# A hybrid decoder layer in fp32: another order of work on TensorE in the mLSTM stage, and a merge that VectorE adds

## The chip, the core and the metric

The kernel runs on one core of one Trainium2 chip. The metric is the time of one execution on the device in microseconds (us), as the median of several runs. The profile comes from one execution of its own, taken by the hardware profiler, with its own time.

The engines are named as the profile names them: PE is TensorE (matmuls; PEld is its weight load), DVE is VectorE, ACT is ScalarE, POOL is GpSimd, SP is SyncE, which issues most DMAs.

## The reference, cut to what matters

One layer on 512 tokens of width 1024. A normalised input feeds two branches, an mLSTM with four heads (branch a) and a sliding-window attention (branch b). Both are projected, gated and added; an output projection, an MLP and a gated embedding follow.

```python
h = rmsnorm(x, norm_mix_g[i])
proj = h @ w_in[i]
...
h_ml = mlstm_chunkwise(q_ml, k_ml, v_ml, ig, lf)          # 4 heads, 128 wide q and k, 256 wide v
h_ml = h_ml * lax.rsqrt(jnp.mean(h_ml * h_ml, axis=-1, keepdims=True) + EPS)
y_a = jax.nn.sigmoid(o_ml) * h_ml * mlstm_norm_g[i]
y_b = swa_with_sinks(q_sw, k_sw, v_sw, sinks[i])
merged = jax.nn.sigmoid(g_a) * (y_a @ w_branch_a[i]) + jax.nn.sigmoid(g_b) * (y_b @ w_branch_b[i])
x = x + merged @ w_out[i]
...
```

## The kernel before, in words

**Arithmetic.** Each fp32 operand of a large product is split into a high and a low part (`split`: ACT casts the high part, DVE subtracts it to get the low part), and the product is three matmuls: high by high, high by low, low by high (`pairs`). One tile of 128 weight columns against all 512 tokens is 8 row blocks times 3, so 24 matmuls of 128x512. One such matmul is called a piece below, the 24 together a column block. `load_w` loads a column block by a DMA of SP's queue and splits it; four pairs of split weights are held (`WB`).

**Stages.** The input projections come first, then the attention (16 units), then the mLSTM with the projection of branch b, then the projection of branch a with the merge, then the output projection, the MLP in four quarters, and the end. The change lies in the mLSTM stage, the merge and the first lines of the output projection.

**The end of the attention.** There PE's order is written out by hand (`manual_schedule` on PE): the last q and k projections are cut into pieces by a generator, and `more(n)` issues n of them between the attention's own products. The last k block ends there; ACT and DVE then run its causal convolution (L671, L673), and `silu` (ACT sigmoid L680, DVE multiply L681) finishes the q and k tiles of all four heads (`acc` in the trace).

**The mLSTM stage.** `ml_weights(h)` makes one head's masked, decayed scores, in four column groups s = 0 to 3 of 512, 384, 256 and 128 tokens. For each group, ACT takes exponentials of 128x128 slices (`dm`, L835, one slice of them from `dg`, which DVE makes at L814), PE makes the score product q by k (L842) in a PSUM bank, DVE multiplies the two (L843), and `split` makes the weights `wT`. `ml_out(h)` multiplies them with the values (`vh`) in four token blocks of 3, 6, 9 and 12 matmuls (30 in all, tile `pst`, L168), ACT copies each result out (L855), DVE takes the denominator (`hd`, `den`, `rd`), and ACT squares the results for the norm (`jk`, L864). `ml_norm` scales the head's result `hs` on DVE (L873) by a root that ACT takes (L259, with a table load before it). `ya_of(h)` turns two blocks of a head on PE (L894), gates them on DVE (`sy`, L895) and splits them into `ya`.

**PSUM.** In this stage PSUM has eight banks: `g` two tiles of a bank for the projections (`psg`), `t` two tiles of a bank (`pst`), `a` two tiles of two banks (`psa`). Scores, products with the values and turned blocks all share the two `t` tiles. A tile's next use waits until its last reader is done.

**Order.** Nothing fixes PE's order here: `branch_b(2h)`, `ml_weights(h+1)`, `ml_out(h)` and `branch_b(2h+1)` are written one after the other, and the framework's scheduler merges them by its own estimates of when each is ready. The order on ACT and DVE is the scheduler's in both kernels. Every engine runs its own list in order.

**Branch b, branch a and merge.** `branch_b(i)` is a column block against `yb`, gated by DVE into `t2[i]` (L882). After the heads, eight column blocks of branch a against `ya` follow; DVE gates each (L920), POOL adds `t2[i]` (L921), and `split` makes `mg`. Then a second set of PSUM tiles takes over the same eight banks: `pair` (three tiles of two banks) for the output projection, allocated first, and `g`.

Of the kernel before, what the change touches and what calls it, by code (L numbers as in the profile page):

```python
# [16 lines left out]
P = 128  # L17
# [20 lines left out]
def block_kernel(  # L38
# [601 lines left out]
    def gate_of(put, i):  # L640

        if i % 2 == 0:
            loaded[0] = sp.tile([P, 2, 512], F32, tag="pT", bufs=2, name=nm("gl"))
            nc.sync.dma_start(out=loaded[0], in_=put[i // 2])
        return loaded[0][:, i % 2, :]

    gbd = gate_proj(w_gb)
    gad = gate_proj(w_ga)
# [87 lines left out]
    def swa_out(kp, gp, n, pTs):  # L736
# [14 lines left out]
        for g in range(2):  # L751
# [5 lines left out]
                o.rearrange("p (m g c) -> p m g c", m=2, g=2)[:, :, g, :],  # L757
            )

    def pieces():  # L760

        order = [("k", 0), ("q", 4), ("q", 5), ("k", 4), ("q", 6), ("q", 7), ("k", 1), ("k", 5), ("k", 2), ("k", 6), ("k", 3), ("k", 7)]
        for kind, i in order:
            w = load_w((w_qsw if kind == "q" else w_qkml)[i], KT * P, KT)
            ps = ps_g()
            for k in range(KT):
                ops = pairs([t[:, k, :] for t in w], hT[k])
                for j, (l, r) in enumerate(ops):
                    T.matmul(ps, l, r, start=k == 0 and j == 0, stop=k == KT - 1 and j == 2)  # L769
                    yield  # L770
            (q_done if kind == "q" else qk_done)(i, ps)

    fill = pieces()

# [32 lines left out]
    def h_of(h, t):  # L807
        return hs[h][t // 2][:, (t % 2) * DV : (t % 2 + 1) * DV]

    def ml_weights(h):  # L810
        pr = sp.tile([P, 512], F32, tag="pr", bufs=2, name=nm("pr"))
        nc.sync.dma_start(out=pr, in_=rrd[h : h + 1, :].broadcast_to([P, 512]))
        dg = act_f("dg")
        V.tensor_tensor(  # L814
            dg.rearrange("p (t j) -> p t j", t=NT),
            pr.rearrange("p (t j) -> p t j", t=NT),
            tri.unsqueeze(1).broadcast_to([P, NT, P]),
            ALU.add,
        )
        if h < 2:  # L820
            room = bp.tile([P, KT, 512], F32R, tag="big", bufs=2, name=nm("wT"))
            w0, w1, l0, l1 = [room[:, k, :] for k in range(4)]
            w2 = [room[:, 4, : 2 * P], room[:, 4, 2 * P :]]
        else:
            w0, w1, l0, l1 = [act_r("wT") for _ in range(4)]
            w2 = [sp.tile([P, 2 * P], F32R, tag="vs", bufs=4, name=nm("wT")) for _ in range(2)]
        wT = [(w0, l0), (w1[:, : 3 * P], l1[:, : 3 * P]), w2, (w1[:, 3 * P :], l1[:, 3 * P :])]
        vhl = [head_values() for _ in range(2)]
        for s in range(NT):
            split([v[:, s, :] for v in vhl], vm[s][:, h, :])  # L830
            dm = act_f("dm")
            n0 = s * P
            for t in range(s, NT):
                src = dg if t == s else pr
                A.activation(  # L835
                    dm[:, t * P : (t + 1) * P],
                    src[:, t * P : (t + 1) * P],
                    AF.Exp,
                    bias=gc[:, t * NT + s, h : h + 1],
                )  # L840
            psc = ps_t()
            T.matmul(psc[:, n0:], qk[4 + h][:, n0 : n0 + P], qk[h][:, n0:], start=True, stop=True)  # L842
            V.tensor_mul(dm[:, n0:], psc[:, n0:], dm[:, n0:])  # L843
            split(wT[s], dm[:, n0:])
        wts[h] = wT, vhl

    def ml_out(h):
        wT, vhl = wts.pop(h)
        for t in range(NT):
            pn = ps_t()  # L850
# [3 lines left out]
            chain(pn[:, : DV + 2], ops, True, True)  # L854
            A.copy(h_of(h, t), pn[:, :DV])  # L855
            V.tensor_copy(hd[:, h, t : t + 1], pn[:, DV : DV + 1])
        den = small("den", NT, 2)
        V.scalar_tensor_tensor(den, hd[:, h, :], -1.0, hd[:, h, :], ALU.mult, ALU.max)
        V.tensor_max(den, den, gc[:, NT * NT :, h])
# [15 lines left out]

    t2 = [None] * 8

    def branch_b(i):
        ps = ps_g()
        mm_T(ps, load_w(w_b[i], KT * P, KT), yb)  # L880
        t2[i] = act_f("gb")
        V.tensor_mul(t2[i], ps, gate_of(gbd, i))  # L882

# [14 lines left out]
    ml_weights(0)  # L898
    rds = []
    for h in range(NH):  # L900
        branch_b(2 * h)
        if h + 1 < NH:
            ml_weights(h + 1)
        rds.append(ml_out(h))
        branch_b(2 * h + 1)
        if h == 1:
            ml_norm([0, 1], rds)
        elif h > 1:
            ml_norm([h], rds[h:])
            ya_of(h - 2)  # L910
    ya_of(2)
    ya_of(3)


    mg = []
    for i in range(8):
        ps = ps_g()
        mm_T(ps, load_w(w_a[i], KT * P, KT), ya)
        sg = act_f("sga")
        V.tensor_mul(sg, ps, gate_of(gad, i))  # L920
        G.tensor_tensor(sg, sg, t2[i], ALU.add)  # L921
        m_ = act_hl("mg")
        split(m_, sg)
        mg.append(m_)


    st_s.close()
# [12 lines left out]
    def ps_g():  # L940
        return pp.tile([P, 512], F32, tag="g", bufs=2, name=nm("psg"))

    def columns_of(dst, k, g):

        ps = pair()[:, 0, :]
        for m in range(NT):
            T.transpose(ps[:, m * P : (m + 1) * P], xk[m][:, k * P : (k + 1) * P], ident)  # L947
        split(dst[k], ps, g[:, k : k + 1])
# [3 lines left out]
    for nh in range(2):  # L952
# [361 lines left out]
```

## Time and profile before

| | |
|---|---|
| Time before, median of 3 runs | 897.93 us (896.87 to 898.82) |
| The profiled execution's own time | 897.05 us |
| Its span (first to last instruction) | 895.3 us |
| PE busy | 884.4 us, 99% of the span |
| DVE busy | 644.8 us, 72% |
| ACT busy | 450.1 us, 50% |
| POOL busy | 24.3 us, 3% |
| Mean granted clock of PE | 0.999 |

The span and the time differ by 1.75 us, which lie outside the instructions. Busy time of PE counts pipelined matmuls with a modelled end: a matmul of 512 columns is drawn 0.39 us long though the next one starts after 0.23 us. So a PE that is 99% busy is one with hardly any gaps, and the length of a stretch is read from starts, not from durations. Idle time that a row names stands in brackets behind it, with the instruction that ended it.

### The profile page before, as it was taken

What the parts mean: (1) busy time and instruction counts of PE and PEld (TensorE: products, weight loads), DVE (VectorE), ACT (ScalarE), POOL (GpSimd) and SP (SyncE); (2) the same over time, 40 slices, a digit from 0 to 9 for tenths busy, and PEclk for the clock granted to TensorE, in tenths of its full rate; (3) what the DMA queues carried; (4) which work ended last, traced back from release to release, by engine and by line L of the source; (5) the groups of instructions that cost most, each with busy time, mean ns of one, the idle gap of its engine ahead of it and who ended that gap; (6) DMA issues with size and microseconds to landing.
All of it is one profiled execution on the core that took longest, in us unless ns stands there. A gap on an engine that the chain in (4) does not pass through costs nothing.

```text
span 895.3 us, 12110 instructions
## 1 busy us (share of the span) xinstructions
PE 884.4 (99%) x4676; PEld 739.9 (83%) x4676; DVE 644.8 (72%) x1029; ACT 450.1 (50%) x757; POOL 24.3 (3%) x42
## 2 busy tenths in 40 slices
PE   9999999999999999999999999999999999999996
PEld 8888899998777777788878888888888888888886
DVE  6875687863877887667634679757966885798566
ACT  6463445443657577765322545334434533444843
POOL 1011000000000000001300000000000000000000
PEclk9999999999999999999999999999999999999999
DMA  7552234345202123335452520630252054102402
GB/s 285 189 176 83 70 118 143 141 137 170 71 24 72 48 94 119 98 114 166 140 189 95 213 70 25 208 109 36 86 197 94 1 169 158 50 25 73 139 1 95
DMA packets 29965, 100.50 MB, mean 112 GB/s; under 512 B 4173, under 2 KB 4685, under 8 KB 29906
## 3 DMA queue, kind: packets, MB, share of 16 engines
q1 hardware_dynamic: 27938, 93.15, 31.4%
q0 software_dynamic: 1824, 6.30, 2.0%
q8 instruction: 37, 0.61, 0.3%
q10 hardware_dynamic: 144, 0.26, 0.1%
q14 instruction: 22, 0.18, 0.1%
HBM read 91.30 MB, written 8.40 MB: 111 GB/s over the span
## 4 chain that ended last, share of the span: by engine, by line
PE 92%; DVE 4%; ACT 3%; issue 0%; POOL 0%; DVEq 0%; POOLq 0%
PE psg L168 45%; PE psp L168 23%; PE psa L168 10%; PE psg L769 4%; PE pst L168 3%; ACT lm L716 1%; PE psa L697 1%; PE psg L319 1%; PE psa L731 1%; DVE acc L673 1%; PE pst L842 1%; PE pst L744 1%; DVE lm L705 1%; PE psp L947 1%; DVE lm L720 1%; PE psg L247 1%
## 5 line engine op out<-in xcount | busy, mean ns | idle before, releaser
L139 ACT CAST wh<-wr 128x1024 fp32r<-128x1024 f32 x134 | 140.6, 1052 | 211.6 <-PE psg L168 61.7
L140 DVE TENSOR_TENSOR wl<-wr,wh 128x1024 fp32r<-128x1024 f32 x134 | 168.5, 1262 | 97.1 <-ACT wh L139 90.1
L168 PE MATMUL psg<-x,wh 128*128 128x512 f32 x512 | 158.3, 390 | 0.0
L168 PE MATMUL psp<-wh,uf 128*128 128x512 f32 x448 | 139.2, 390 | 0.0
L168 PEld LDWEIGHTS psg<-x,wh 128*128 128x128 f32 x512 | 96.1, 188 | 19.7
L168 PE MATMUL psg<-x,wl 128*128 128x512 f32 x256 | 99.7, 389 | 0.0
L168 PEld LDWEIGHTS psp<-wh,uf 128*128 128x128 f32 x448 | 84.1, 188 | 17.3
L168 PE MATMUL psp<-wl,uf 128*128 128x512 f32 x224 | 87.2, 389 | 0.0
L139 ACT CAST wh<-wd 128x1024 fp32r<-128x1024 f32 x44 | 46.3, 1054 | 57.4 <-PE psp L168 25.8
L769 PE MATMUL psg<-h,wh 128*128 128x512 f32 x192 | 61.6, 397 | 0.4 <-DVE acc L673 0.4
L140 DVE TENSOR_TENSOR wl<-wd,wh 128x1024 fp32r<-128x1024 f32 x44 | 53.4, 1218 | 4.4 <-ACT wh L139 4.1
L168 PEld LDWEIGHTS psg<-x,wl 128*128 128x128 f32 x256 | 48.1, 188 | 9.9
L168 PE MATMUL psa<-h,wh 128*128 128x256 f32 (+1 forms) x256 | 55.1, 311 | 0.0
L168 PEld LDWEIGHTS psp<-wl,uf 128*128 128x128 f32 x224 | 42.1, 188 | 8.7
L140 DVE TENSOR_TENSOR uf<-F,uf 128x1792 fp32r<-128x1792 f32 (+2 forms) x20 | 33.0, 1651 | 21.8 <-ACT uf L139 21.8
L168 PEld LDWEIGHTS psa<-h,wh 128*128 128x128 f32 x256 | 41.9, 191 | 3.5 <-ACT p L618 0.8
L168 PE MATMUL psg<-yb,wh 128*128 128x512 f32 x128 | 43.0, 408 | 0.3 <-DVE gb L882 0.2
L769 PEld LDWEIGHTS psg<-h,wh 128*128 128x128 f32 x192 | 35.6, 188 | 7.8 <-ACT pT L733 0.8
L716 ACT ACTIVATE lm<-lm,nmx 128x256 f32<-128x256 f32 (+1 forms) x64 | 30.0, 470 | 23.6 <-DVE nmx L709 23.6
L139 ACT CAST uf<-F 128x1792 fp32r<-128x1792 f32 (+2 forms) x20 | 27.9, 1397 | 26.3 <-DVE F L1023 26.2
L168 PE MATMUL psg<-ya,wh 128*128 128x512 f32 x128 | 40.6, 395 | 0.0
L1009 DVE SCALAR_TENSOR_TENSOR rt<-psg,rB 128x512 f32<-128x512 f32 x32 | 22.0, 689 | 25.6 <-PE psg L168 25.6
(289 smaller groups left out, 1745.1 us busy)
## 6 DMA issues: line engine op xcount, KB each, us to landing
wr<-in_w_up SPq DMA_DIRECT2D x32, 512.0 KB, 3.5
wd<-in_w_down SPq DMA_DIRECT2D x24, 512.0 KB, 4.3
wr<-in_w_o SPq DMA_DIRECT2D x8, 512.0 KB, 4.0
gd<-gr POOLq DMA_DIRECT2D x8, 512.0 KB, 3.4
wr<-in_w_qsw SPq DMA_DIRECT2D x8, 512.0 KB, 4.3
wr<-in_w_qkml SPq DMA_DIRECT2D x8, 512.0 KB, 3.3
wr<-in_w_b SPq DMA_DIRECT2D x8, 512.0 KB, 3.4
gl<-gd SPq DMA_DIRECT2D x8, 512.0 KB, 3.4
```

The costliest lines, as they stand in the source:

```text
L139: done = A.copy(dst[0], src)
L140: V.tensor_sub(dst[1], src, r32(dst[0]))
L168: last_mm[0] = T.matmul(ps, l, r, start=first and i == 0, stop=last and i == len(ops) - 1, skip_group_check=parts)
L247: tc.keep_in_program_order(T.matmul(idle[:, :P], ones, ones, start=True, stop=True))
L319: last_mm[0] = T.matmul(ps[:, :264], act, w, start=done == 0, stop=done == 3 * KT - 1)
L673: V.scalar_tensor_tensor(acc[:, s:], ps[:, : S - s], cw[:, i * 4 + 3 - s : i * 4 + 4 - s], acc[:, s:], ALU.mult, ALU.add)
L697: T.matmul(o, q[x][HALF[ab], n * P : (n + 1) * P], keys[kp][y][HALF[ab], k0 : k0 + 256], start=i == 0, stop=i == 2)
L705: V.tensor_tensor_reduce(lm3[:, g, :], ls[:, g * 256 : g * 256 + W], band[:, 256 - W :], 0.125, sk[:, g // 2, g % 2 : g % 2 + 1], ALU.add, ...
L716: A.activation(lm3[:, g, :], lm3[:, g, :], AF.Exp, bias=nmx[:, g : g + 1], accum_out=sm[:, g : g + 1])
L720: V.tensor_tensor(lm3, lm3, rc.unsqueeze(2).broadcast_to([P, 4, W]), ALU.mult)
L769: T.matmul(ps, l, r, start=k == 0 and j == 0, stop=k == KT - 1 and j == 2)
L1009: V.scalar_tensor_tensor(a, ps, 0.0, rB, ALU.max, ALU.mult)
```

## The change

The edit has four parts.

1. The mLSTM stage gets a written order on PE. The projection of branch b, and the first two column blocks of branch a, become a generator of 240 pieces (`branches`), which `more(n)` places between the heads' own products: 6 behind each score of head 0, 5 behind each score of the other heads, 4 behind each token block of an output, 8 behind the turned blocks of heads 0 and 1, 44 behind those of head 2, and the last 32 behind those of head 3. `ml_weights(0)` comes first, ahead of any piece.
2. The score products go to the `a` tiles (two tiles, of which one bank each is used) and no longer share the `t` tiles.
3. In the merge DVE adds the two branches (`a_done`), where POOL did.
4. The second set of PSUM tiles allocates its two `g` tiles first, so that they take the banks of the old `g` tiles and the `pair` tiles take the others. They serve the second half of the output projection.

The loaded gates are kept by their source, since branch a and b now alternate.

```diff
-    def ml_weights(h):
+    def ml_weights(h, n):
...
-            psc = ps_t()
+            psc = ps_a()[:, :512]
             T.matmul(psc[:, n0:], qk[4 + h][:, n0 : n0 + P], qk[h][:, n0:], start=True, stop=True)
             V.tensor_mul(dm[:, n0:], psc[:, n0:], dm[:, n0:])
             split(wT[s], dm[:, n0:])
+            more(n)
...
-    def branch_b(i):
-        ps = ps_g()
-        mm_T(ps, load_w(w_b[i], KT * P, KT), yb)
+    def branches():
+
+        for i in range(8):
+            yield from pieces_of(w_b[i], yb, lambda ps: b_done(i, ps))
+        for i in range(2):
+            yield from pieces_of(w_a[i], ya, lambda ps: a_done(i, ps))
...
+    def a_done(i, ps):
+        sg = act_f("sga")
+        V.tensor_mul(sg, ps, gate_of(gad, i))
+        V.tensor_add(sg, sg, t2[i])
+        mg.append(act_hl("mg"))
+        split(mg[i], sg)
+
+    fill = branches()
     rds = []
-    for h in range(NH):
-        branch_b(2 * h)
...
+    with tc.manual_schedule(engines={mybir.EngineType.PE}):
+        ml_weights(0, 6)
+        for h in range(NH):
+            if h + 1 < NH:
+                ml_weights(h + 1, 5)
+            rds.append(ml_out(h, 4))
+            if h == 1:
+                ml_norm([0, 1], rds)
+            elif h > 1:
+                ml_norm([h], rds[h:])
+                ya_of(h - 2)
+                more(8)
+        ya_of(2)
+        more(44)
+        ya_of(3)
+        for _ in fill:
+            pass
...
-        G.tensor_tensor(sg, sg, t2[i], ALU.add)
...
+    first_g = [ps_g(), ps_g()]
...
-            pv = [a[:, 0, :], a[:, 1, :], ps_g(), ps_g()]
+            pv = [a[:, 0, :], a[:, 1, :], *first_g]
```

**PE at the start of the stage.** `pst_3418` is the last product of the attention, `acc_2332` and `acc_2642` are q and k of head 0, `yb` marks a piece of branch b. Before:

```order
L744 MATMUL pst_3418<-pT_3399,vs_358 64x256 x2
L168 MATMUL psg_3520<-yb_2433,wh_3523 128x512
L168 MATMUL psg_3520<-yb_2434,wh_3523 128x512
L168 MATMUL psg_3520<-yb_2433,wl_3524 128x512
...
L168 MATMUL psg_3520<-yb_3342,wh_3523 128x512
L842 MATMUL pst_3485<-acc_2332,acc_2642 128x512
L842 MATMUL pst_3496<-acc_2332,acc_2642 128x384
L168 MATMUL psg_3520<-yb_3343,wh_3523 128x512
```

And of the changed kernel:

```order
L744 MATMUL pst_3418<-pT_3399,vs_358 64x256 x2
L846 MATMUL psa_3487<-acc_2332,acc_2642 128x512
L766 MATMUL psg_3498<-yb_2433,wh_3494 128x512
...
L766 MATMUL psg_3498<-yb_2437,wl_3495 128x512
L846 MATMUL psa_3511<-acc_2332,acc_2642 128x384
...
L846 MATMUL psa_3527<-acc_2332,acc_2642 128x256
L766 MATMUL psg_3498<-yb_3034,wh_3494 128x512
```

Nineteen pieces stood ahead of the first score; now none does, and six stand between one score and the next.

**ACT ahead of the scores of head 3.** `vh_3887` are the values of head 3, `jk` the squares of head 1, `dm_3891` the first exponentials of head 3, `wh_4222` a weight cast. Of the changed kernel:

```order
L139 CAST vh_3887<-vm_840 128x258
L139 CAST wh_4222<-wr_4220 128x1024
L870 ACTIVATE jk_3858,hss<-hs_3463,rd_3856 128x256
L839 ACTIVATE dm_3891<-pr_3877,gc 128x128
L870 ACTIVATE jk_3858,hss<-hs_3463,rd_3856 128x256
L839 ACTIVATE dm_3891<-dg_3879,gc 128x128
L870 ACTIVATE jk_3858,hss<-hs_3464,rd_3856 128x256
```

Squares and exponentials alternate, as they do in part in the kernel before; on PE the third score of head 3 is now ten pieces behind the first, where it was 28 pieces behind the second.

## Rows read from the trace of the kernel before

**Rows 1.** The page, first part: busy time, share, instructions of each engine.

```profile
PE 884.4 (99%) x4676; PEld 739.9 (83%) x4676; DVE 644.8 (72%) x1029; ACT 450.1 (50%) x757; POOL 24.3 (3%) x42
```

**Rows 2.** Timeline of PE, 331 to 350 us: start, length, operation, count, [idle before].

```profile
331.30 1.95 PE L744 MATMUL pst<-pT,vs 128*64 128x256 f32 x16
333.18 0.73 PE L168 MATMUL psg<-yb,wh 128*128 128x512 f32 x2
...
337.62 1.66 PE L842 MATMUL pst<-acc,acc 128*128 128x512 f32 x4
...
346.97 1.77 PE L842 MATMUL pst<-acc,acc 128*128 128x512 f32 x4 [0.38 <-DVE dm L843]
```

**Rows 3.** Timeline of DVE and ACT around the first scores of head 0.

```profile
336.44 0.68 DVE L681 SCALAR_TENSOR_TENSOR acc<-acc,sg 128x512 f32<-128x512 f32 x1
336.75 2.20 ACT L680 ACTIVATE sg<-acc 128x512 f32<-128x512 f32 x4
340.98 0.68 DVE L814 TENSOR_TENSOR dg<-pr,tri 128x512 f32<-128x512 f32 x1
341.32 1.28 ACT L835 ACT_TABLE_LOAD   x1
...
342.92 0.39 ACT L835 ACTIVATE dm<-dg,gc 128x128 f32<-128x128 f32 x1
343.22 0.68 ACT L835 ACTIVATE dm<-pr,gc 128x128 f32<-128x128 f32 x2
343.93 0.69 DVE L843 TENSOR_TENSOR dm<-pst,dm 128x512 f32<-128x512 f32 x1 [1.13 <-ACT dm L835]
```

**Rows 4.** Timeline of ACT and PE around the outputs of heads 0 and 1.

```profile
361.17 0.51 ACT L864 ACTIVATE jk<-hs,rd 128x256 f32<-128x256 f32 x1
361.98 0.49 ACT L864 ACTIVATE jk<-hs,rd 128x256 f32<-128x256 f32 x1
364.20 0.62 ACT L139 CAST wT<-dm 128x512 fp32r<-128x512 f32 x1 [0.76 <-DVE dm L843]
369.60 4.00 PE L168 MATMUL pst<-vh,wT 128*128 128x258 f32 x30
373.52 0.41 ACT L139 CAST vh<-vm 128x258 fp32r<-128x258 f32 x1 [0.97 <-PE pst L168]
375.58 0.51 ACT L864 ACTIVATE jk<-hs,rd 128x256 f32<-128x256 f32 x1 [0.46 <-DVE rd L861]
```

**Rows 5.** Timeline of PE, ACT and DVE around the scores of head 3.

```profile
376.20 1.66 PE L842 MATMUL pst<-acc,acc 128*128 128x512 f32 x4
376.73 1.03 ACT L139 CAST wh<-wr 128x1024 fp32r<-128x1024 f32 x1
380.66 0.30 ACT L259 ACTIVATE sd<-hss,eps_t 128x8 f32<-128x8 f32 x1
381.43 2.19 DVE L873 TENSOR_SCALAR hs<-hs,rs 128x256 f32<-128x256 f32 x8
384.27 0.70 PE L842 MATMUL pst<-acc,acc 128*128 128x256 f32 x2
```

**Rows 6.** Timeline of DVE: the gate of a turned block.

```profile
409.56 0.74 DVE L895 SCALAR_TENSOR_TENSOR sy<-pst,gml,gl 128x512 f32<-128x512 f32 x1
```

**Rows 7.** Timeline, all engines: branch a's last column block and the output projection's start.

```profile
445.26 0.62 PE L168 MATMUL psg<-ya,wh 128*128 128x512 f32 x2
...
450.48 0.39 PE L168 MATMUL psg<-ya,wl 128*128 128x512 f32 x1
450.90 0.69 DVE L920 TENSOR_TENSOR sga<-psg,gl 128x512 f32<-128x512 f32 x1 [1.63 <-PE psg L168]
451.74 0.47 PE L168 MATMUL psp<-wh,mg 128*128 128x512 f32 x1 [0.88 <-ACT wh L139]
```

**Rows 8.** Busy time of each engine in stretches at the end; PEclk is the granted clock.

```profile
core 0: us, PE busy (x) PEld busy (x) DVE busy (x) ACT busy (x) POOL busy (x), PEclk, DMA share, GB/s
885.00:890.00 5.00, 3.11 (x26) 2.90 (x25) 3.93 (x14) 3.35 (x6) 0.00 (x0) 1.00 0.29 108
893.00:895.30 2.30, 0.00 (x0) 0.00 (x0) 0.00 (x0) 0.00 (x0) 0.00 (x0) 0.50 0.23 86
```

More of the change, by code (lines that the diff above doesn't have):

```diff
@@ L642, in gate_of @@
         if i % 2 == 0:
-            loaded[0] = sp.tile([P, 2, 512], F32, tag="pT", bufs=2, name=nm("gl"))
-            nc.sync.dma_start(out=loaded[0], in_=put[i // 2])
-        return loaded[0][:, i % 2, :]
+            loaded[id(put)] = sp.tile([P, 2, 512], F32, tag="pT", bufs=2, name=nm("gl"))
+            nc.sync.dma_start(out=loaded[id(put)], in_=put[i // 2])
+        return loaded[id(put)][:, i % 2, :]
     gbd = gate_proj(w_gb)
@@ L758, in swa_out, with pieces_of @@
             )
+    def pieces_of(src, acts, done):
+        w = load_w(src, KT * P, KT)
+        ps = ps_g()
+        for k in range(KT):
+            ops = pairs([t[:, k, :] for t in w], acts[k])
+            for j, (l, r) in enumerate(ops):
+                T.matmul(ps, l, r, start=k == 0 and j == 0, stop=k == KT - 1 and j == 2)
+                yield
+        done(ps)
     def pieces():
@@ L763, in pieces @@
         for kind, i in order:
-            w = load_w((w_qsw if kind == "q" else w_qkml)[i], KT * P, KT)
-            ps = ps_g()
[L766 to L771, printed above, removed]
+            done = q_done if kind == "q" else qk_done
+            yield from pieces_of((w_qsw if kind == "q" else w_qkml)[i], hT, lambda ps: done(i, ps))
     fill = pieces()
@@ L844, in ml_weights, with ml_out @@
             split(wT[s], dm[:, n0:])
+            more(n)
         wts[h] = wT, vhl
-    def ml_out(h):
+    def ml_out(h, n):
         wT, vhl = wts.pop(h)
@@ L856, in ml_out @@
             V.tensor_copy(hd[:, h, t : t + 1], pn[:, DV : DV + 1])
+            more(n)
         den = small("den", NT, 2)
@@ L876, in block_kernel, with b_done @@
     t2 = [None] * 8
-    def branch_b(i):
-        ps = ps_g()
-        mm_T(ps, load_w(w_b[i], KT * P, KT), yb)
+    def branches():
[3 more added lines that the diff above has]
+            yield from pieces_of(w_a[i], ya, lambda ps: a_done(i, ps))
+    def b_done(i, ps):
         t2[i] = act_f("gb")
@@ L896, in ya_of @@
             split(ya[i], sg)
-    ml_weights(0)
-    rds = []
-    for h in range(NH):
-        branch_b(2 * h)
[L902 to L916, printed above, removed]
+    mg = []
+    def a_done(i, ps):
[5 more added lines that the diff above has]
+    fill = branches()
+    rds = []
+    with tc.manual_schedule(engines={mybir.EngineType.PE}):
[15 more added lines that the diff above has]
+            pass
+    for i in range(2, 8):
         ps = ps_g()
         mm_T(ps, load_w(w_a[i], KT * P, KT), ya)
-        sg = act_f("sga")
-        V.tensor_mul(sg, ps, gate_of(gad, i))
-        G.tensor_tensor(sg, sg, t2[i], ALU.add)
-        m_ = act_hl("mg")
-        split(m_, sg)
-        mg.append(m_)
+        a_done(i, ps)
     st_s.close()
```

## The prediction

> **What bounds the kernel now.** I read the page first: PE is busy for 884.4 of 895.3 us [rows 1]. So PE bounds it, and the change can gain no more than PE's gaps in the stretch that it touches, while every gap that it opens there is lost for good: the amount of work on PE is the same before and after. Next I read PE's timeline through the stretch, 333 to 452 us. The pace of a piece is read from starts: the last column block of branch a goes from 445.26 to 450.48 in 23 steps, 0.227 us each [rows 7]. By that pace PE hardly ever stops in the mLSTM stage; the gaps to be seen are 0.38 us at 346.97 [rows 2] and 1.03 us at the change to the output projection: the last piece starts at 450.48, is over by 450.71, and the next matmul starts at 451.74 [rows 7]. Then I read DVE and ACT in the same stretch, since they feed the scores, and asked when each input is ready, not how busy they are.
>
> **What PE's stages cost.** A row's length has a modelled tail of 0.39 - 0.227 = 0.16 us. The first two scores of a head take 1.66 - 0.16 = 1.50 us [rows 2], by width 0.86 and 0.64; the third and fourth then 0.43 and 0.21. A head's 30 output matmuls take 4.00 - 0.16 = 3.84 us [rows 4].
>
> **Part 1, the order on PE.** It adds no work. It removes the scheduler's freedom to put a ready piece ahead of a score that waits: everything behind that score on PE's list waits with it, and nothing else on the chip needs PE's answer sooner for it. So I walked down the new list with the row lengths.
>
> *First score.* It reads q and k of head 0 after `silu`. The second of these multiplies starts at 336.44 and lasts 0.68, so it ends at 337.12 [rows 3], behind the last convolution on DVE, whose order up to there is unchanged. The attention's last products leave PE free at 333.18, where now a piece of branch b starts [rows 2]. Before, pieces filled the time up to 337.62; now the score is first in line. Wait: 337.12 - 333.18 = 3.9 us.
>
> *Third score of head 0.* There are two tiles for scores, so the third one waits until DVE has multiplied the first. PE gets there after 0.86 + 6 x 0.227 + 0.64 + 6 x 0.227 = 4.2 us, at 341.3. ACT's sigmoids end at 338.95 and its table load takes 1.28, but the slice made from `dg` waits for DVE until 340.98 + 0.68 = 341.66; from the start of that slice to the end of the two after it are 343.22 + 0.68 - 342.92 = 0.98 us, then the multiply takes 0.69 [rows 3]: 343.3. Wait: 2.0 us. The fourth score has its tile at about 344.3 and PE comes at 345.1, so it does not wait; nor do those of head 1, where ACT and DVE are about 1.5 us ahead. PE ends head 0's scores at 346.7, those of head 1 (2.14 + 20 x 0.227) at 353.4, and the output of head 0 (3.84 + 12 x 0.227, with 4 more pieces behind it) at 359.9.
>
> *Head 2.* Its exponentials stand on ACT between the squares of head 0, which wait for that output. From the output's end to the first square are 375.58 - 373.52 = 2.06 us, and a square with a slice of exponentials takes 361.98 - 361.17 = 0.81 [rows 4]. So: 359.9 + 2.06 + 4 x 0.81 + 0.1 + 0.69 = 366.0. PE stands before the third score at 359.9 + 0.91 + 0.86 + 1.14 + 0.64 + 1.14 = 364.6. Wait: 1.4 us. The fourth score needs the second multiply, a cast of 0.62 [rows 4], 0.98 and about 0.55 later, at 368.15, and PE comes at 367.6: 0.6 us.
>
> *Head 3.* With 0.21 + 1.14 + 3.84 + 12 x 0.227 the output of head 1 ends at 376.1, and PE is before the third score at 380.8. ACT now also has a weight cast of 1.03 us [rows 5] ahead of the squares; part of it lies in the wait of 2.06, so it costs between 0 and 1.03, and I take 0.55: 376.1 + 2.6 + 3.35 + 0.69 = 382.7. Wait: 1.9 us. Between the first and second multiply DVE then has the norm of heads 0 and 1: a table load (1.28) and, from the start of the root to the end of the scaling, 381.43 + 2.19 - 380.66 = 2.96 us [rows 3, 5]; then a low part, a gate and the multiply, about 1.9 in all. From the exponentials' end at 382.0 that is 388.1, and PE comes at 384.3: 3.8 us.
>
> *Outputs and turned blocks.* The outputs have their weights a head ahead, and four pieces (0.91 us) between two token blocks cover ACT's copy out of the tile. I price them at nothing; without that cover each of 16 would cost some tenths. The last wait is at `ya_of(3)`: behind its turned blocks only two pieces can go before one needs the new block. The gate takes 0.74 [rows 6] and a cast 0.62 [rows 4], 1.36 against some 0.9 of two pieces and four transposes (an estimate, taking these at the length of the pieces): 0.5 us; the low part, behind a second gate, costs about as much again. Together 1.0 us.
>
> Sum of the waits: 3.9 + 2.0 + 1.4 + 0.6 + 1.9 + 3.8 + 1.0 = 14.6 us. Where a chain has many links, an instruction starts a little before the recorded end of the one ahead (343.22 against 342.92 + 0.39 [rows 3]), about 0.09 a link; over some ten links in the waits that are set by chains I take off 0.8, which leaves 13.8 us.
>
> **Part 2, other banks for the scores.** The products with the values no longer share tiles with scores, so a score does not wait for a copy out. But it is still two tiles, and the wait for the first multiply stays, as reckoned above. The gap of 0.38 at 346.97, a score waiting for the multiply two scores earlier [rows 2], goes as that gap, since the time there is part of the walk.
>
> **Part 3, the add on DVE.** It puts eight more DVE instructions of about 0.69 us (the length of the gate next to it [rows 7]) into column blocks of 5.46 us each, where DVE waits 1.63 us for PE already [rows 7]. Nothing.
>
> **Part 4, the banks.** The wait at 451.74 is put down to ACT, but DVE's gate of the last column block ends at 450.90 + 0.69 = 451.59 [rows 7], and it reads the bank that the first new tile takes. With the banks exchanged the first matmul needs only banks long free, so I book the whole 1.03 us as gained; if the weight cast is what ended it, nothing is gained.
>
> **Sum.** 13.8 - 1.03 - 0.38 = 12.4 us more. On the profiled execution's own time of 897.05 that is 909.5. The median of the runs lies 0.9 above it, so I forecast 910.4 us.
>
> **The rivals.**
>
> *A. The chains of heads 2 and 3 keep up.* PE's waits push the outputs later, but ACT and DVE have slack too; if the squares and exponentials come some 4 us sooner than my walk has them, only the first score, the third one and the last turned blocks wait: 3.9 + 2.0 + 1.0 - 1.4 = 5.5 more, 903.4. For it: the two engines idle in this stretch. Against it: in the kernel before the third score of head 3 came 384.27 - 376.20 = 8.1 us after the first [rows 5], and PE was filling up pieces then, not holding the chain back.
>
> *B. The clock falls in the first wait.* At the end of the kernel PE is busy for 3.11 us of the stretch that begins at 885, and by 893 its granted clock is at 0.50, 1.2 GHz instead of 2.4 [rows 8]; so a PE without work loses its clock there, and the first wait leaves it without work for 3.9 us. If it fell then, the 4.2 us of work between first and third score would take up to 8.4; the 2.0 us of the wait behind them cover a part, so 2.2 more: 912.6. Against it: in that idle end PE stays without work for longer than in the wait. The Trainium skill (TensorE: Matmul & The Clock Gate, section "HAM oscillation — how this bites in real kernels") tells of a kernel whose PE waits for data between bursts and finds the clock at half rate at each new burst, which speaks for this rival; no gap in the middle of this trace is long enough to test it.
>
> *C. No score ever waits long (the other side).* If the multiply for head 0 were done by 333.2, and each score were read within the 4.2 us that PE needs from one score to the next but one, all the waits would be covered and only the gaps of before would go: 897.9 - 1.4 = 896.5. The point from which it decides is that distance of 4.2 us; the rows give 337.12 for the multiply [rows 3] and 8.1 us for head 3 [rows 5]. That the order isn't what the change says is excluded by the list.
>
> **How the numbers follow.** Forecast 0.67, A 0.16, B 0.10, C 0.04, and 0.03 for something worse than B. The weight cast (0 to 1.03), the gain at the banks (0 to 1.03), the links' overlap and the outputs' cover move the forecast by some 3 us each way, 907 to 914. The range reaches down to A and up past B, 902 to 915, and leaves out C, the edges of A and the worst. About 0.2% is what a measurement can tell from no change here: faster 0.04, within it 0.02, slower 0.94.
>
> **What would show it.** In the trace after, PE's first score should start near 337.1 with some 4 us of idle time before it that end with DVE's `acc` multiply; the third score of head 0 should wait about 2 us for DVE's `dm` multiply; the third and fourth scores of head 3 should show 2 and 4 us. The chain of waits should get more DVE and ACT. The gap before the first `psp` matmul should be gone. The prediction is wrong if `silu` is done by 333, or if the third scores start without idle time; with a clock below 1 after 337 it is rival B.

## The result

The changed kernel takes 909.97 us as the median of five runs (908.21 to 912.3). The kernel before took 898.27 us beside it (896.87 to 898.82, five runs, the three of the table above among them). The ratio is 1.0137, 95% interval 1.0116 to 1.0157, so the change makes the kernel 1.4% slower. The forecast was 910.4, with a range of 902 to 915. The profiled execution of the changed kernel took 909.97 with a span of 908.0. On another chip the ratio was 1.0134 [1.0119, 1.0149].

### The profile page after: what moved, and what is told of

It is laid out like the page before. It is cut to its first block, busy times and chain, and to the rows that moved or that the text cites. A ratio compares the mean times of both kernels' runs of the same rounds, so it can differ in the third digit from the quotient of the medians.

```text
span 908.0 us, 12108 instructions
## 1 busy us (share of the span) xinstructions
PE 886.7 (98%) x4676; PEld 742.1 (82%) x4676; DVE 645.3 (71%) x1037; ACT 450.3 (50%) x757; POOL 12.2 (1%) x34
## 4 chain that ended last, share of the span: by engine, by line
PE 89%; DVE 6%; ACT 4%; DMA 1%; issue 0%; SPq 0%; POOL 0%; ACTq 0%; POOLq 0%
PE psg L168 38%; PE psp L168 23%; PE psa L168 10%; PE psg L766 9%; PE pst L168 3%; ACT lm L716 1%; DVE acc L673 1%; PE psa L697 1%; PE psg L319 1%; PE psa L731 1%; DMA xt<-in_x 1%; DVE lm L705 1%; PE psp L966 1%; DVE lm L720 1%; PE pst L744 1%; DVE wl L140 1%
## 5 line engine op out<-in xcount | busy, mean ns | idle before, releaser
L140 DVE TENSOR_TENSOR wl<-wr,wh 128x1024 fp32r<-128x1024 f32 x134 | 163.2, 1221 | 96.9 <-ACT wh L139 90.0
L766 PE MATMUL psg<-h,wh 128*128 128x512 f32 x192 | 61.6, 397 | 0.4 <-DVE acc L673 0.4
L168 PE MATMUL psa<-h,wh 128*128 128x256 f32 (+1 forms) x256 | 55.2, 312 | 0.0
L766 PE MATMUL psg<-yb,wh 128*128 128x512 f32 x128 | 45.6, 429 | 0.0
L168 PE MATMUL psg<-h,wh 128*128 128x512 f32 x128 | 39.9, 393 | 0.0
```

The lines of the kernel that those rows point to most:

```text
L140: V.tensor_sub(dst[1], src, r32(dst[0]))
L168: last_mm[0] = T.matmul(ps, l, r, start=first and i == 0, stop=last and i == len(ops) - 1, skip_group_check=parts)
```

## The profile after

The page's first part: busy time, share and instructions of each engine, against [rows 1].

```profile
PE 886.7 (98%) x4676; PEld 742.1 (82%) x4676; DVE 645.3 (71%) x1037; ACT 450.3 (50%) x757; POOL 12.2 (1%) x34
```

PE has as many instructions as before in a span that is 12.7 us longer. POOL has eight instructions less, DVE eight more: the adds. The waits of PE say where the time is (engine, tile and line, what it waits for: us in total, times, longest us):

```profile
PE psa L846 <- DVE dm L847: 6.5, 4, 3.4
PE psa L846 <- DVE acc L681: 4.0, 1, 4.0
PE psg L766 <- ACT ya L139: 0.6, 1, 0.6
PE psg L766 <- DVE ya L140: 0.2, 1, 0.2
```

That is 11.3 us in seven waits, all of them in the rewritten stage, which had two gaps of 0.58 us in all before (0.38 us [rows 2], and 0.20 us at 360.40). Their places stand in PE's timeline (start, length, operation, count, [idle before]). L846 is the line of the scores, and each row with x2 is a score of 512, 384, 256 or 128 tokens.

```profile
331.54 1.95 PE L744 MATMUL pst<-pT,vs 128*64 128x256 f32 x16
...
337.51 1.10 PE L846 MATMUL psa<-acc,acc 128*128 128x512 f32 x2 [4.02 <-DVE acc L681]
...
343.70 0.70 PE L846 MATMUL psa<-acc,acc 128*128 128x256 f32 x2
...
366.55 0.70 PE L846 MATMUL psa<-acc,acc 128*128 128x256 f32 x2 [1.25 <-DVE dm L847]
368.68 0.49 PE L846 MATMUL psa<-acc,acc 128*128 128x128 f32 x2 [0.28 <-DVE dm L847]
...
383.10 0.70 PE L846 MATMUL psa<-acc,acc 128*128 128x256 f32 x2 [1.64 <-DVE dm L847]
388.32 0.49 PE L846 MATMUL psa<-acc,acc 128*128 128x128 f32 x2 [3.37 <-DVE dm L847]
...
464.19 0.39 PE L168 MATMUL psg<-ya,wl 128*128 128x512 f32 x1
464.41 0.39 PE L168 MATMUL psp<-wh,mg 128*128 128x512 f32 x1
```

The rows to compare are the first ones of [rows 2], the third score of head 3 in [rows 5] and the last two of [rows 7]. The first score waits 4.02 us, as forecast; the third score of head 0 shows no wait; those of heads 2 and 3 do; and the gap of 1.03 us ahead of the output projection is gone (464.19 to 464.41 is the pace of a piece).

One more thing differs: the clock. Busy time in stretches of 2 us (us, then busy time of PE, PEld, DVE, ACT and POOL, then PEclk, the granted clock, then DMA):

```profile
338.00:340.00 2.00, 2.00 (x6) 1.42 (x5) 2.00 (x4) 1.98 (x4) 0.00 (x0) 0.63 0.46 186
340.00:342.00 2.00, 2.00 (x6) 1.32 (x4) 1.90 (x4) 0.94 (x3) 0.00 (x0) 0.52 0.01 2
342.00:344.00 2.00, 1.93 (x8) 1.24 (x7) 0.86 (x2) 2.00 (x7) 0.00 (x0) 1.00 0.00 0
...
388.00:390.00 2.00, 1.68 (x8) 1.42 (x9) 1.25 (x4) 1.50 (x4) 0.00 (x0) 0.93 0.60 178
390.00:392.00 2.00, 2.00 (x8) 1.71 (x7) 0.98 (x4) 0.98 (x3) 0.00 (x0) 0.50 0.21 84
392.00:394.00 2.00, 2.00 (x10) 1.82 (x10) 1.55 (x2) 1.42 (x2) 0.00 (x0) 0.72 0.00 0
```

Behind each of the two longest waits the granted clock falls to about 0.50, the 1.2 GHz of its two levels (a stretch in which it changes shows a value between). The first two rows lose 0.37 x 2 + 0.48 x 2 = 1.7 us of work at full speed; the second fall loses as much over the last three rows. The first one explains why the third score shows no wait: PE took 6.2 us from the first score to the third (337.51 to 343.70), where the walk has 4.2.

**The account by starts.** The last score of head 3 starts 56.8 us after the attention's last group (388.32 - 331.54); before it was 56.1, from this row to the first of [rows 2].

```profile
387.35 0.38 PE L842 MATMUL pst<-acc,acc 128*128 128x128 f32 x2
```

So the chain of scores and outputs ends at nearly the same time. But PE has run 111 pieces by then (24 + 20 + 16 + 20 + 16 + 15, as the order is written), where it had run 159 before (counted in the trace). The 48 missing pieces are 10.9 us at 0.227 us, and they are run behind that point instead. With the 0.7 us by which the score itself is later, 0.8 for the turned blocks and 1.7 for the clock behind the last score, less 1.03, that makes 13.1. Measured from the attention's last group to the first `psp` matmul it is 12.4 (464.41 - 331.54 against 451.74 - 331.30 [rows 2, 7]); of the rest of 0.7, 0.2 is the second fall, which cost 1.5 by starts and not 1.7 (shown at the end of the experiments), and 0.5 I can't place.

## The experiments

The theory was the prediction's: PE waits because its list leaves it no other work, and the waits end when ACT and DVE are ready. Rivals were that the score tiles or the add carry the loss, or that ACT and DVE bound the stage so that filling one wait opens another.

**Parts of the change alone.** Three kernels keep the scheduler's order. The first has only the banks of the output projection:

```diff
+    first_g = [ps_g(), ps_g()]
...
-            pv = [a[:, 0, :], a[:, 1, :], ps_g(), ps_g()]
+            pv = [a[:, 0, :], a[:, 1, :], *first_g]
```

> The kernel before, with only the new layout of the second set of PSUM tiles (its g tiles allocated first, and used in the second half of the output projection). Theory (the gap of 1.03 us at the change to the output projection waits for the gate that reads the old bank): the gap is gone, 897.2 us against 898.3. Rival (the weight cast that the profile names ends it): 898.3 and the gap still there.

Measured: 896.4 against 897.42, ratio 0.9989 [0.9981, 0.9998], and the first matmul of the output projection has no idle time before it:

```profile
451.10 0.39 PE L168 MATMUL psp<-wh,mg 128*128 128x512 f32 x1
```

So the gate that read the old bank ended the gap, not the weight cast that the profile names. Part 4 brings the 1.0 us that it was booked at, with an interval of 0.2 to 1.7. The second has everything but the written order (the gates kept by their source, and the two column blocks of branch a between the heads, belong to that order):

```diff
-            psc = ps_t()
+            psc = ps_a()[:, :512]
...
-        G.tensor_tensor(sg, sg, t2[i], ALU.add)
+        V.tensor_add(sg, sg, t2[i])
...
+    first_g = [ps_g(), ps_g()]
...
-            pv = [a[:, 0, :], a[:, 1, :], ps_g(), ps_g()]
+            pv = [a[:, 0, :], a[:, 1, :], *first_g]
```

> Everything of the change but the written order: the scheduler orders PE as before, scores in the a tiles, DVE adds in the merge, the output projection's banks as in the change. Theory (all of the loss is the order): the gap before the output projection goes, 1.0, and the one of 0.38 before a score may go; the add costs nothing: 898.3 - 1.0 = 897.3, at best 896.9. Rival (the two a tiles for the scores or the add on DVE carry a part of the loss): 900 or more.

Measured: 895.27 against 897.48, ratio 0.9977 [0.9966, 0.9987]. So the other three parts together gain 2.2 us, and the order alone costs the step from 0.9977 to 1.0137, 14 us. The third leaves the add on POOL:

```diff
-            psc = ps_t()
+            psc = ps_a()[:, :512]
...
+    first_g = [ps_g(), ps_g()]
...
-            pv = [a[:, 0, :], a[:, 1, :], ps_g(), ps_g()]
+            pv = [a[:, 0, :], a[:, 1, :], *first_g]
```

> The kernel before with the two parts on PSUM alone: scores in the a tiles, and the output projection's banks as in the change; POOL adds in the merge, as before. Theory (the add on DVE is free, and the last experiment under the scheduler's order gained 1.0 by the banks and the rest by the score tiles): the same as with the add, 895.3 to 896. Rival (the add made a part of that gain): 896.4, as the banks alone. Another rival (the add costs something that the other parts cover): below 894.5.

Measured: 894.75 against 897.47, ratio 0.9968 [0.9956, 0.9981], the lowest of this study. The intervals with and without the add overlap: no price of the add can be told. The score tiles are worth more than the 0.38 us that I gave them. By the step from 0.9989 to 0.9968 it is about 1.9, by starts in the traces 1.3: the last score comes 3.7 us earlier than with the `t` tiles, and PE's gaps of 0.38 and 0.20 us are gone. What the rest of the 1.3 us is, no row shows as a wait.

```profile
383.75 0.38 PE L842 MATMUL psa<-acc,acc 128*128 128x128 f32 x2
```

**One wait filled: 19 pieces ahead of the first score.**

```diff
+        more(19)
         ml_weights(0, 6)
...
-        more(44)
+        more(25)
```

> The changed kernel, with 19 of its 44 late pieces put ahead of the first score. Theory (the time is in the waits of the written order): the first score starts at about 337.3 as now, but PE works until then, so the wait of 4.0 us and the fall of the clock behind it are gone; the third score of head 0 then waits its full 2.0 us, so everything up to head 3 keeps its time and 19 pieces x 0.227 = 4.3 us are saved behind it: 905.7 us against 910.0. Rival (PE's waits are only a sign: ACT and DVE bound the whole stage, and the time comes back as a wait at the turned blocks): 909 to 910.

Measured: 908.67 (908.48 to 909.93) against 897.42, ratio 1.0128. PE's timeline:

```profile
338.15 1.02 PE L846 MATMUL psa<-acc,acc 128*128 128x512 f32 x2
...
344.59 0.70 PE L846 MATMUL psa<-acc,acc 128*128 128x256 f32 x2 [2.00 <-DVE dm L847]
...
389.41 0.80 PE L846 MATMUL psa<-acc,acc 128*128 128x128 f32 x2 [3.90 <-DVE dm L847]
...
423.34 0.49 PE L766 MATMUL psg<-ya,wh 128*128 128x512 f32 x1 [1.54 <-ACT ya L139]
```

The first wait is gone and the clock stays at 1.00 there, but only about 1 of 4 us is won, which the two intervals, 1.0116 to 1.0157 and 1.0114 to 1.0142, do not tell from nothing. The third score now waits 2.00 us, the term of the prediction that the slow clock had hidden. The last score waits 0.5 longer, the turned blocks 0.9 longer, and the low clock behind the last score takes about twice as much, 3.4 us by the stretches from 388 to 396, of which one reads:

```profile
392.00:394.00 2.00, 2.00 (x7) 1.68 (x7) 0.67 (x3) 0.43 (x2) 0.00 (x0) 0.50 0.00 0
```

My expectation had left all of these as they were; the rival was nearer.

**No score tile to wait for.** Four one-bank tiles for scores take the place of the two `a` tiles of two banks:

```diff
-            psc = ps_a()[:, :512]
+            psc = ps_s()
...
+    def ps_s():
+        return pp.tile([P, 512], F32, tag="s", bufs=4, name=nm("pss"))
```

> The changed kernel, with the scores in four PSUM tiles of one bank each, where it has two tiles; order untouched. Theory (third and fourth scores wait for the multiply of the score two before): the waits of 1.25, 0.28, 1.64 and 3.37 us in heads 2 and 3 go, with them the second fall of the clock (half of 3.4 us, 1.7), while the first wait of 4.0 us stays with its fall; the clock's loss there is no longer covered by the third score's wait. 910.0 - 6.5 - 1.7 = 901.8, up to 2 us more if PE then comes too early to an output. Rival (the scores' waits only move to the outputs, which need the same multiplies): 908 to 910.

Measured: 908.74 (908.35 to 909.45), ratio 1.0124.

```profile
338.71 2.04 PE L849 MATMUL pss<-acc,acc 128*128 128x512 f32 x2 [4.01 <-DVE acc L682]
...
373.83 1.34 PE L169 MATMUL pst<-vh,wT 128*128 128x258 f32 x9 [0.58 <-DVE hd L864]
...
388.69 0.73 PE L769 MATMUL psg<-yb,wh 128*128 128x512 f32 x2 [1.45 <-DVE gb L896]
...
392.30 2.27 PE L169 MATMUL pst<-vh,wT 128*128 128x258 f32 x9 [2.42 <-DVE hd L864]
```

No score waits for a tile any more, and 4.45 us of waits stand behind the scores instead, three of them: two at output blocks whose tile DVE has still to read, one at a piece whose tile it has still to gate. The rival held: the wait is not the tile's, it is that of a PE that is ahead of ACT and DVE.

**The norm moved.** The root and the scaling of heads 0 and 1 stand between the first two multiplies of head 3. This kernel takes them with the norm of head 2, and turns heads 0 and 1 behind the output of head 3:

```diff
-            if h == 1:
-                ml_norm([0, 1], rds)
-            elif h > 1:
-                ml_norm([h], rds[h:])
-                ya_of(h - 2)
+            if h == 2:
+                ml_norm([0, 1, 2], rds)
+                more(8)
+            elif h == 3:
+                ml_norm([3], rds[3:])
+                ya_of(0)
+                ya_of(1)
                 more(8)
```

> The changed kernel with one step of ACT and DVE moved: the norm of heads 0 and 1 is taken together with that of head 2, behind the output of head 2, and their turned blocks come behind the output of head 3. So ACT has no table load and no root between the two first groups of head 3's exponentials, and DVE no scaling between its first and second multiply. Theory (the last score of head 3 waits 3.37 us because the norm stands in front of the multiply it waits for): that wait falls to between 0 and 0.5, and the fall of the clock behind it goes, 1.7 us; 910.0 - 3.1 - 1.7 = 905.2. Rival (the pace of ACT and DVE as a whole sets the end of this stretch, so the wait only moves to the outputs or the turned blocks): 908 to 910.

In the changed kernel, DVE's timeline shows what the last score waits for: the multiply at 387.71 stands behind the root's reciprocal, the scaling, a low part and a gate.

```profile
382.36 0.69 DVE L847 TENSOR_TENSOR dm<-psa,dm 128x512 f32<-128x512 f32 x1 [1.71 <-ACT dm L839]
383.97 0.20 DVE L261 RECIPROCAL rs<-sd 128x8 f32<-128x8 f32 x1 [0.92 <-ACT sd L259]
384.20 0.23 DVE L877 TENSOR_TENSOR rs<-rs,rd 128x4 f32<-128x4 f32 x2
384.40 2.19 DVE L879 TENSOR_SCALAR hs<-hs,rs 128x256 f32<-128x256 f32 x8
...
387.71 0.55 DVE L847 TENSOR_TENSOR dm<-psa,dm 128x384 f32<-128x384 f32 x1
```

With the norm moved, PE's timeline reads:

```profile
386.33 0.49 PE L846 MATMUL psa<-acc,acc 128*128 128x128 f32 x2 [0.60 <-DVE dm L847]
...
403.91 1.70 PE L168 MATMUL pst<-vh,wT 128*128 128x258 f32 x12 [1.88 <-DVE hd L861]
```

Its wait fell from 3.37 to 0.60 us, just above the 0 to 0.5 expected. But the time is 910.11 (909.28 to 910.54), ratio 1.0139: nothing is won. The scaling, now 3.23 us long and behind head 2, stands on DVE in front of the copy that an output block of head 3 waits for, 1.88 us:

```profile
400.56 3.23 DVE L879 TENSOR_SCALAR hs<-hs,rs 128x256 f32<-128x256 f32 x12
403.71 0.21 DVE L861 COPY hd<-pst 128x1 f32<-128x1 f32 x2
```

That the norm ends the wait is shown; that moving it pays is refuted.

**Pieces where the waits are.** Two kernels move many pieces at once, still in a written order. Cut to the lines ahead of the last score of head 3, the first is:

```diff
-        ml_weights(0, 6)
+        more(19)
+        ml_weights(0, (6, 15, 6, 6))
...
+        ml_weights(2, (5, 11, 6, 5))
...
+        ml_weights(3, (5, 11, 14, 3))
```

> The changed kernel, still in a written order, with 53 pieces taken from places behind the last score of head 3 and put ahead of the places where PE waited: 19 ahead of the first score, 9 more ahead of the third score of head 0, 6 and 1 more ahead of the third and fourth of head 2, 6 and 9 more ahead of the third and fourth of head 3; the two column blocks of branch a take turns, so that enough pieces are left ahead of the last turned blocks. Theory (the loss is where the pieces stand, and ACT and DVE reach the last score of head 3 at the same time whatever PE does meanwhile): the waits of 11.4 us shrink to about 1, and the clock no longer falls, 1.9: 910.0 - 10.4 - 1.9 = 897.7, level with the kernel before. Rival (half of what is gained comes back as later chains, as with the 19 pieces alone): 902 to 905.

Measured: 904.08 (903.47 to 904.41), ratio 1.0074 [1.0057, 1.0091]; the clock does not fall. Ahead of the last score stand 50 pieces more than in the changed kernel, which is what the places listed above add up to, not 53. Four of its waits:

```profile
389.41 0.49 PE L846 MATMUL psa<-acc,acc 128*128 128x128 f32 x2 [1.83 <-DVE dm L847]
393.74 1.35 PE L168 MATMUL pst<-vh,wT 128*128 128x258 f32 x9 [1.60 <-DVE hd L861]
398.44 0.66 PE L911 MATMUL pst<-ident,hs 128*128 128x128 f32 x4 [1.01 <-DVE hd L861]
...
416.44 0.50 PE L766 MATMUL psg<-ya,wh 128*128 128x512 f32 x1 [1.25 <-DVE ya L140]
```

The scores' waits fall from 10.6 to 2.3 us. But this kernel has one piece between two blocks of the outputs of heads 2 and 3, where the changed one has four, and lets branch a's first two column blocks take turns; 5.3 us of waits stand at those outputs and the turned blocks, where there were 0.8. So half of what I expected came, and the time lies in the rival's range. The second kernel moves 21 more, of which the diff against the first one shows the largest part:

```diff
-        ml_weights(3, (5, 11, 14, 3))
-        rds.append(ml_out(2, 1))
+        ml_weights(3, (5, 11, 21, 0))
+        rds.append(ml_out(2, (1, 8, 1, 3)))
```

> The written order of the last experiment with pieces, with 21 of the 24 pieces that stood ahead of the last turned blocks (12 stay there, counted with the turns of branch a) put where that run still waited: 7 more ahead of the last score of head 3 (1.83 us there), 7 more ahead of the third token block of head 2's output (1.60), 2 ahead of the fourth score of head 2 (0.45), 2 behind that output (1.01), 2 in head 3's output (0.61); branch a's two column blocks alternate by six pieces. Theory (all the loss is a matter of how many pieces stand ahead of each waiting point; the last turned blocks are ready at 413, about 6 us before PE came to them): some 5 of the 7.6 us of waits go, and the waits behind the last turned blocks (0.83 and 1.25) shrink by half: 904.1 - 6 = 898, level with the kernel before. Rival (the chain behind the last score moves later as fast as the waits are filled, or the turned blocks wait now): 901 to 904.

Measured: 901.78 (901.26 to 903.11), ratio 1.0048 [1.0033, 1.0064]. The waits at 389 and 393 are filled; a new one is there, with the clock falling behind it. First PE and its clock, then the gate on DVE that it waits for:

```profile
392.31 0.79 PE L766 MATMUL psg<-yb,wh 128*128 128x512 f32 x1 [2.12 <-DVE gb L899]
```

```profile
392.00:394.00 2.00, 1.69 (x7) 1.59 (x8) 1.11 (x3) 0.79 (x3) 0.00 (x0) 0.54 0.83 250
```

```profile
391.57 0.69 DVE L899 TENSOR_TENSOR gb<-psg,gl 128x512 f32<-128x512 f32 x1
```

DVE's list has that gate behind the second multiply and two low parts; PE, with its pieces put earlier, needs the gate's PSUM tile before DVE comes to it. My expectation fell short again, and by the same cause: a filled wait brings PE sooner to the next one.

Together the runs give this, each time from the start of the attention's last matmul (1.6 us behind the start of its last group, from which the account above counts) by PE's starts:

| kernel | pieces ahead of head 3's last score | that score, us | output projection begins, us | ratio |
|---|---|---|---|---|
| before | 159 | 54.5 | 118.9 | 1 |
| changed | 111 | 55.2 | 131.3 | 1.0137 |
| 19 pieces first | 130 | 56.0 | 130.0 | 1.0128 |
| four tiles | 111 | 49.4 | 129.8 | 1.0124 |
| norm moved | 111 | 52.5 | 130.0 | 1.0139 |
| pieces where waits are | 161 | 56.4 | 125.0 | 1.0074 |
| pieces again | 168 | 56.0 | 123.2 | 1.0048 |
| scheduler, score tiles, banks | 143 | 50.7 | 116.4 | 0.9968 |

The score's time does not tell the result, and neither do the pieces alone; what counts is how much work PE has done by then. With four tiles the last score comes 5.8 us earlier and with the norm moved 2.7, but with the same 111 pieces done, and the output projection begins only 1.5 and 1.3 us earlier. In the last row the score comes 3.8 us earlier than before with 16 pieces fewer, which are 3.6 us, and nothing is lost. Between the changed kernel and the row of pieces again, 57 more pieces cut 8 of the 12.4 us, with the score's time 0.8 us later. No run writes the scheduler's own order out by hand; the 4.3 us by which that row is still later than before stand against 4.4 us of waits and one fall of the clock in its trace.

**The clock.** Matmuls whose results nobody reads (`useless`) keep PE busy in the two longest waits, 17 ahead of the first score and 14 ahead of the last one of head 3:

```diff
+    def useless(n):
+        ps = ps_t()
+        for i in range(n):
+            T.matmul(ps, yb[0][0][:, :P], yb[0][0], start=True, stop=True)
...
+            if (h, s) == (0, 0):
+                useless(17)
+            if (h, s) == (3, 3):
+                useless(14)
```

> The changed kernel, with useless matmuls of 512 columns where PE waits longest: 17 ahead of the first score (3.9 us) and 14 ahead of the last score of head 3 (3.2 us); their result is read by nobody. PE waits for the same things as before, but works meanwhile. Clock theory: the granted clock stays at 1.00 all through; at the first place nothing is gained, since the third score of head 0 then waits about 2 us; at the second place the half rate of 389.7 to 393.1 us goes and 1.7 us are gained: 908.3 against 910.0. Rival (the waits alone make the time and the recorded clock costs nothing): 910.0 or a little more.

Measured: 908.08 (907.89 to 908.43), ratio 1.0119 [1.0105, 1.0132], and the span is 906.1 where the changed kernel had 908.0. The granted clock stays at 1.00. With the first fall away, the third score's wait is there:

```profile
343.48 0.70 PE L855 MATMUL psa<-acc,acc 128*128 128x256 f32 x2 [1.68 <-DVE dm L856]
...
388.08 0.49 PE L855 MATMUL psa<-acc,acc 128*128 128x128 f32 x2 [0.19 <-DVE dm L856]
```

Then each place by itself, with the same `useless`, and the changed kernel again without an edit, on one chip. Ahead of the first score alone:

```diff
+            if (h, s) == (0, 0):
+                useless(17)
```

> The changed kernel with the 17 unread matmuls of 512 columns ahead of the first score alone. Theory (the first fall of the clock costs nothing, since the third score would have waited for its multiply in the same time): the clock stays at 1.00 behind the first score, the third score of head 0 waits 1.7 again, the second fall at 390 stays, and the time is that of the changed kernel. Rival (each fall costs half of its 3.4 us): 1.7 us less than the changed kernel on the same chip.

Ahead of the last score of head 3 alone:

```diff
+            if (h, s) == (3, 3):
+                useless(14)
```

> The changed kernel with the 14 unread matmuls ahead of the last score of head 3 alone. Theory (behind that score PE has its whole list ready, so the second fall is paid in full, 3.4 us at half rate): 1.7 us less than the changed kernel on the same chip, and no wait that grows. Rival (a later wait, at the last turned blocks, takes it up): less than 0.6 us.

And the changed kernel:

> The changed kernel as it is, on the same chip as the two kernels with unread matmuls in one place each, so that 1 to 2 us can be told. By the two theories: the same as with the unread matmuls ahead of the first score, 1.7 us more than with those ahead of the last.

Measured, against 897.53: unread work first 909.11 (907.78 to 910.43), last 909.28 (908.54 to 909.98), the changed kernel 909.48 (908.59 to 910.68). Three medians within 0.4 us tell none of the theories apart, and the reason is in the traces: the falls come and go between executions. In this execution of the changed kernel the clock is low behind the first wait only, and longer:

```profile
338.00:340.00 2.00, 2.00 (x5) 1.11 (x4) 2.00 (x4) 1.98 (x3) 0.00 (x0) 0.50 0.57 231
340.00:342.00 2.00, 2.00 (x6) 1.54 (x5) 1.59 (x3) 0.94 (x4) 0.00 (x0) 0.50 0.00 0
...
390.00:392.00 2.00, 2.00 (x15) 1.79 (x14) 1.60 (x6) 1.65 (x5) 0.00 (x0) 1.00 0.31 121
```

The kernel with unread work first has, in its profiled execution, the wait of 3.37 us and no fall behind it, as the granted clock shows:

```profile
388.00:390.00 2.00, 2.00 (x12) 1.73 (x12) 1.25 (x4) 1.76 (x6) 0.00 (x0) 1.00 0.82 254
390.00:392.00 2.00, 2.00 (x14) 1.75 (x13) 1.70 (x5) 1.70 (x4) 0.00 (x0) 1.00 0.02 8
```

Its four runs lie in pairs: 907.8 and 907.9 with a mean clock of 0.998, and 910.4 twice with 0.995 and 0.996. The gain of 1.7 us that I expected of the unread work ahead of the last score did not come, 0.2 by the medians. In the repeat of the changed kernel, though, four runs at one mean clock, 0.994, lie between 908.59 and 910.68. So the mean clock does not tell what a fall cost. By the ratios 1.0134 and 1.0119, whose intervals overlap, the clock takes 1.3 us over the executions, and 1.9 by the two spans.

The traces tell the two falls apart where the medians don't. From the last score of head 3 to the first `psp` matmul PE has the same work in five executions. It took 76.1 us in the first one of the changed kernel, with the second fall (388.32 to 464.41), and 74.6 in the four without it: both places filled, the last one filled, the changed kernel's repeat, and unread work first. The last two, in this order, have the wait of 3.37 us:

```profile
388.58 0.49 PE L846 MATMUL psa<-acc,acc 128*128 128x128 f32 x2 [3.37 <-DVE dm L847]
...
463.19 0.39 PE L168 MATMUL psp<-wh,mg 128*128 128x512 f32 x1
```

```profile
387.79 0.49 PE L853 MATMUL psa<-acc,acc 128*128 128x128 f32 x2 [3.37 <-DVE dm L854]
...
462.41 0.39 PE L168 MATMUL psp<-wh,mg 128*128 128x512 f32 x1
```

So the second fall cost 1.5 us in the one of these executions that has it. From the attention's last group to that score the same comparison gives the price of the first: 56.8 us with the fall of the changed kernel's first execution and 56.8 without a fall (both places filled, and unread work first), but 57.4 with the longer fall of the repeat and of the kernel with the last place filled. So the first fall cost nothing in one execution and 0.6 us in two.

## Why the prediction was right

**First score.** Forecast 3.9 us, ended by the multiply at 337.12; measured 4.02, with the score at 337.51. Right.

**Third score of head 0.** Forecast 343.3 with a wait of 2.0. It started at 343.70, but without a wait, since rival B happened as well. With the clock held up the wait is 1.68, and with 19 pieces first 2.00. The walk was right; what it met was a slower PE (6.2 us from the first score to the third, not 4.2).

**Heads 2 and 3.** Forecast 1.4, 0.6, 1.9 and 3.8; measured 1.25, 0.28, 1.64 and 3.37, each somewhat shorter, 1.2 us together. The 0.8 that I took off the sum for overlapping links foresaw a part of that. The cause of the 3.8, the norm in front of the multiply, is confirmed by the run that moves it. Rival A, that the chains keep up, fell.

**Turned blocks and outputs.** Forecast 1.0 and nothing; measured 0.82 and nothing. The cover of four pieces between output blocks may matter: in the kernel with one piece there, waits of 1.60 and 1.01 us stand at and behind an output, but that kernel moved other pieces too.

**Parts 2 to 4.** The banks gave the 1.03 us in full, as far as an interval of 0.2 to 1.7 can tell. The add costs nothing that can be told. The score tiles were mis-sized: I gave them 0.38 us, and under the scheduler's order they give 1.3 to 1.9. The two gaps of before are 0.58 of that; that scores no longer stand in line with the outputs for two tiles would explain the rest, but no run shows it apart. In the written order that gain cannot be seen.

**The clock.** Rival B had a chance of 0.10 and a price of 2.2 us. That chance was too low: the profiled execution of the changed kernel shows two falls and its repeat one. The price of 2.2 was too high: where the fall was short the wait of the third score covered all of it, and where it was longer 0.6 us were left. A fall behind the last score, 1.5 us in the one execution that has it, I had not considered. The argument against B, that the idle end [rows 8] is longer, was a poor one: it showed that a long gap suffices, not that 4 us don't. The Trainium skill (TensorE: Matmul & The Clock Gate, section "HAM oscillation — how this bites in real kernels") tells of a kernel whose matmuls start at half rate behind each of its waits for data. Here that held behind the gap of 4.0 us in both profiled executions of the changed kernel, and behind the gap of 3.37 us in one of them.

**The sum.** The walk had 14.6 us of waits, 13.8 with the overlap taken off. The profiled execution has 11.4 as waits and 1.7 as slow clock in the place of the third score's wait, 13.1 together. So the walk was 0.7 too long, and the second fall of 1.5, which it did not have, is above that. That the forecast of 910.4 and the median of 909.97 lie 0.4 us apart is therefore in part luck: terms of opposite signs, a rest that I can't place, and five runs that lie between 908.21 and 912.3. The two slowest of these, 911.75 and 912.3, have a mean clock of 0.991 where the others have 0.994 and 0.995; no trace of them is kept, so where their clock fell stays open. What the prediction said of the mechanism, a PE that waits at the places of its list where ACT and DVE are not ready, is what the traces show.

## What to carry to other kernels

Where PE runs a list in order and is the bound, count the work that the list puts ahead of each point at which PE must wait for another engine, not the latency of that engine: here nearly the same time of the chain on ACT and DVE (54.5 and 55.2 us) cost nothing with 159 pieces ahead of its end, and 12 us with 111. Filling one wait moves PE to the next point sooner, so the waits have to be walked through together, with the order on the other engines' lists, before an order is written by hand. And the parts of a change should be run without its largest part: the two changes of PSUM tiles alone beat both kernels, the kernel before by 0.3%.

## What was not expected of the hardware

The same wait of 3.37 us on PE, at the same place of the same program, was followed by a granted clock of 0.50 in one execution and of 1.00 in another. Behind the wait of 4.0 us the clock fell in every profiled execution that had it, five of them; of the two of the changed kernel, one was back at 1.00 by 342 us, and the other had 0.88 at 342 to 344. The length of the wait does not settle it either: in the last kernel with pieces moved a wait of only 2.12 us was followed by 0.54, and with four score tiles one of 2.42 by 0.58. Runs of one kernel differ by up to 4.1 us (908.21 to 912.3), which is more than the step between some of the kernels compared here; the clock is a part of that, and whether it is all of it is not shown.
